# Weights of v and u of the first head pair loaded with q's and k's, and convolution parameters read as the twelfth step, in a hybrid decoder step

## The chip, the core and the metric

The kernel runs on one core of a Trainium2 chip. It is written in a tile framework whose scheduler decides, ahead of the run, in which order each engine's instructions stand; at run time every engine works through its own queue in that order. The engines are TensorE (PE, matrix products; its weight loads are shown as PEld), VectorE (DVE), ScalarE (ACT), GpSimd (POOL) and SyncE (SP), which issues nearly all DMAs. The metric is the device time of one execution in microseconds (us). Before the change the median of three runs is 2768.96 us (2768.74 to 2772.76).

## What is computed

One step of a decoder layer for a prompt of 2048 tokens (with 16 meta tokens ahead of it) and for 8 sampled tokens with paged caches. A normalised input h goes through one projection into q, k, v (8 heads of 64) and u (512 channels); q, k and v feed a stick-breaking attention, u a pooling mixer; their outputs go through one output projection, and a gated FFN with a causal convolution of width 3 follows.

```python
h = rmsnorm(xp, norm_mix_g)
q, k, v, u = project_mix(h, w_in)          # h @ w_in, cut into four
k_prompt, v_prompt = k, v                  # also outputs
...
o_attn = stick_breaking(q, k, v, ...)      # A = sigmoid(z) * prod(1 - sigmoid(z)), z = q k^T * scale + bias
o_pool = multiscale_pool(u, 0, T, pool_w, pool_scale)
xp = xp + concat([o_attn, o_pool]) @ w_out
h2 = rmsnorm(xp, norm_ffn_g)
f, conv_prompt = conv_ffn(h2, zero_prefix, w_up, conv_w, conv_b, w_down)
y_prompt = rmsnorm(xp + f, norm_final_g)
```

## The kernel before

All is float32. A product is done as three products of split values: `split` (L159) casts a tile to a high part on ScalarE (L160) and subtracts on VectorE for the low part (L161); `mm3` (L163) then runs high x high, high x low and low x high (L166 to L168).

**The input projection** is tiled by g, one of four head pairs (128 channels each of q, k, v and u), and by ch, one of four chunks of 512 tokens. `prep_first` loads the four x tiles of chunk 0 (`xt`), squares them (L209), works out 1/rms (`rstd_from`), scales them on VectorE (L232), and `turned` transposes them (`tpx`, L222) into eight tiles `hk` with high and low part (L225, L226), which are also written to DRAM (`hs_s`, L228). For chunks 1 to 3 the same is done in two parts while g is 0: `prep_squares` loads and squares four x tiles (`xt`, rooms shared with the attention's `om`), and `prep_piece` loads a quarter of the columns again as `xp` (L259), scales and turns it. `prep_small` does it for the 24 rows of sampled and meta tokens.

`step(g, ch, ki)` projects one of q, k, v, u (ki 0 to 3) for one g and ch. With ch 0 and ki 0 or 2 it first calls `load_w` for two kinds (the weights `wr`, two rooms, split into `wh` and `wl`), and `few_rows`, which multiplies the 24 small rows by the unsplit weights (L302), turns the result (`tq`, L307) and writes it out. `project` runs 24 products of 512 columns into one of two banks (`psm`), copies them out (`kf`, L384) and writes q and k to DRAM (`q_s`, `k_s`, L386); k and v are turned once more (`pk`, L353) and go to the outputs from `ko` (L357). For u the window sums become `dT`. At ch 1, ki 3, `fold_pool` multiplies the pooling's weights into part of w_out (`pkf`, `pkw`, L395 and L402, with a tile `wt` of w_out), and scales with one column group of `par`.

`room` (L195) gives one of four shared tiles (`kf`, `sm`, `qt`, `dT`, `wt` and others).

**The attention** runs in units of a block of 128 queries and up to 512 keys. `fetch` reads k and q back from DRAM (`raw` and `qr`, L469, L457, L458; `vtm` and `vt` for v, L481, L487; six `vt` rooms of 256 KB) and splits them; `chain` computes `z` (L518), two sigmoids (L519, L520) and a scan along the keys on VectorE (L527), `turn` transposes and `weigh` multiplies by v (`po`, L615).

**The order** is set in two ways. A list `fill` holds the steps of the input projection and, behind them, those of the output projection. Between attention units as many steps of `fill` are called as the next units need, and at least as many as spread the list's input part evenly over three quarters of the units. `with_params`, the second of `fill`, reads the convolution's parameters and the pooling's scale (`ra`, `rb`; turned as `pkp`, L636, L637, into `par`) and the state of the pooling (`sp`; turned as `pkg`, L642, and summed into `spool`). In that order of calls the framework's scheduler then places the instructions on the engines, by its own estimate of when each is ready.

The convolution's part of `par` is not read before the FFN; `fold_pool` reads the pooling's scale from it; `few_rows` for v and u reads `spool`.

Of the kernel before, what the change touches and what calls it, by code (L numbers as in the profile page):

```python
# [9 lines left out]
F32 = mybir.dt.float32  # L10
# [4 lines left out]
ALU = mybir.AluOpType  # L15
# [46 lines left out]
def hymba_kernel(  # L62
# [96 lines left out]
    def split(hi, lo, src):  # L159
        nc.scalar.copy(hi, src)  # L160
        nc.vector.tensor_tensor(out=lo, in0=src, in1=f32(hi), op=ALU.subtract)  # L161
# [122 lines left out]
        nc.vector.tensor_tensor(out=hsml[:, :, 0:n], in0=tp[:, :, 0:n], in1=gcol.unsqueeze(2).broadcast_to([P, NK, n]),  # L284
                                op=ALU.mult)

    def load_w(g, kind):
        ft = 4 * "qkvu".index(kind) + g
        wr = pa.tile([P, NK, P], F32, name="wr", bufs=2)
        nc.sync.dma_start(out=wr, in_=w_in[:, ft * P:(ft + 1) * P].rearrange("(c p) f -> p c f", p=P))  # L290
        wh = pa.tile([P, NK, P], F32R, name="wh", bufs=4)
        wl = pa.tile([P, NK, P], F32R, name="wl", bufs=4)
        split(wh, wl, wr)
        return wh, wl, wr

    def few_rows(g, pair, w):

        cs = slice(g * P, (g + 1) * P)
        ps = tt_tile("t24")[:, 0, :]
        for c in range(NK):  # L300
            for j in range(2):
                nc.tensor.matmul(ps[32 * j:32 * j + 32, :], hsml[:, c, :], w[pair[j]][2][:, c, :],  # L302
                                 start=c == 0, stop=c == NK - 1, skip_group_check=True)
        sm = room("sm")[:64, 0:P]
        nc.scalar.copy(sm, ps[:64, :])
        tq = tt_tile("tq")[:, 0, 0:64]
        nc.tensor.transpose(tq, sm, ident[:64, :64])  # L307
        mt = pb.tile([P, P], F32, name="mt", tag="ot")[:, 0:64]
        nc.vector.tensor_copy(mt, tq)
        if pair == "qk":  # L310
            qt = room("qt")[:NS, 0:P]
            nc.vector.tensor_scalar(out=qt, in0=sm[0:NS, :], scalar1=SCALE, scalar2=None, op0=ALU.mult)
            nc.sync.dma_start(out=qd_s[:, cs], in_=qt)
            nc.sync.dma_start(out=k_sample[:, cs], in_=sm[32:32 + NS, :])
            nc.sync.dma_start(out=k_prompt[0:META, cs], in_=sm[32 + NS:32 + NS + META, :])
            nc.sync.dma_start(out=q_s[g][:, 0:META], in_=mt[:, NS:NS + META])
            nc.sync.dma_start(out=k_s[g][:, 0:META], in_=mt[:, 32 + NS:32 + NS + META])
            return
        nc.sync.dma_start(out=v_sample[:, cs], in_=sm[0:NS, :])
        nc.sync.dma_start(out=v_prompt[0:META, cs], in_=sm[NS:NS + META, :])  # L320
        nc.sync.dma_start(out=pool_sample[:, 14, cs], in_=sm[32:32 + NS, :])
        us, um = mt[:, 32:32 + NS], mt[:, 32 + NS:32 + NS + META]
        ut = pa.tile([P, META], F32, name="utail", bufs=2)
        tails[g] = ut
        nc.vector.tensor_copy(ut, um)
        ub = room("ubm")
        nc.vector.memset(ub[:, 0:META], 0.0)
        nc.vector.tensor_copy(ub[:, META:2 * META], um)
        src = window_sums(ub, g, 2 * META)
        dT = room("dTm")  # L330
        nc.vector.tensor_tensor(out=src[:, META:2 * META], in0=src[:, META:2 * META], in1=invc[:, g, :], op=ALU.mult)
        nc.vector.tensor_tensor(out=dT[:, NS:NS + META], in0=src[:, META:2 * META], in1=um, op=ALU.subtract)
        nc.vector.tensor_tensor(out=dT[:, 0:NS], in0=spool[:, g, :], in1=us, op=ALU.add)
        nc.vector.scalar_tensor_tensor(out=dT[:, 0:NS], in0=dT[:, 0:NS], scalar=1.0 / WIN[g], in1=us,
                                       op0=ALU.mult, op1=ALU.subtract)
        nc.sync.dma_start(out=cat_s[4 + g, :, 0:NS + META], in_=dT[:, 0:NS + META])
# [67 lines left out]
            nc.scalar.copy(wf, pk)  # L404
            nc.sync.dma_start(out=wf_s[g * P:(g + 1) * P, q * CW:(q + 1) * CW], in_=wf)

    w = {}

    def step(g, ch, ki):

        pair = "qkvu"[ki // 2 * 2:ki // 2 * 2 + 2]
        if ch == 0 and ki % 2 == 0:
            for kind in pair:
                w[kind] = load_w(g, kind)
            few_rows(g, pair, w)
        nxt = (ch + 1) % NCH
        ahead = ki == 3 and (g < 3 if ch == NCH - 1 else g > 0)
# [207 lines left out]
            if end:  # L625
                end()

    def with_params():
        ra, rb, sp = room("ra")[:, 0:P], room("rb")[:NPR - P, 0:P], room("sp")[:15 * NS, 0:512]
        cw = conv_w.rearrange("i (f p) -> (i f) p", p=P)  # L630
        nc.sync.dma_start(out=ra, in_=cw[0:P, :])
        nc.sync.dma_start(out=rb[0:4, :], in_=cw[P:132, :])
# [3 lines left out]
        nc.tensor.transpose(tp[:, 0:P], ra, ident)  # L636
        nc.tensor.transpose(tp[:, P:NPR], rb, ident[:NPR - P, :NPR - P])  # L637
        nc.vector.tensor_copy(par, tp)
        nc.sync.dma_start(out=sp, in_=state_pool.rearrange("b j f -> (b j) f"))
        for g, w in enumerate(WIN):  # L640
            tg = tt_tile("pkg").rearrange("p a b -> p (a b)")[:, 0:15 * NS]
            nc.tensor.transpose(tg, sp[:, g * P:(g + 1) * P], ident[:15 * NS, :15 * NS])  # L642
            nc.vector.tensor_reduce(out=spool[:, g, :],
                                    in_=tg.rearrange("p (b j) -> p b j", j=15)[:, :, 16 - w:],
                                    axis=AX.X, op=ALU.add)


    wo, out_pool = [], {}
# [48 lines left out]
    for fn, key in in_steps():  # L697
        fill.append(fn)
        if key:
            ready[key] = len(fill)  # L700
        if len(fill) == 1:
            fill.append(with_params)
    n_in = len(fill)
    fill += [lambda c=c: load_out(c) for c in range(NK)]
    heads = [attention(hp) for hp in range(4)]
# [547 lines left out]
```

## Time and profile before

| | us |
|---|---|
| median of 3 runs | 2768.96 (2768.74 to 2772.76) |
| the profiled execution: whole time | 2771.54 |
| the profiled execution: span, first to last instruction | 2769.8 |
| TensorE busy | 2662.7 (96%) |
| VectorE / ScalarE / GpSimd busy | 1805.2 / 1031.4 / 721.7 |

The mean granted clock of TensorE is 0.988 of its full speed. By stretches the input projection and the attention take the first 890 us or so, and the output projection's last tiles, the FFN and the sampled rows the rest, in which TensorE is busy for 1859 of 1880 us.

A row of a timeline is: start, length, engine, line, operation, output<-input, partitions x elements, and in brackets how long the engine was idle before the row and what it waited for. SPq is the queue of DMA issues on SP: its start is the time of the issue, not of the landing.

### The profile page before, as it was taken

The numbers are of one execution on the slowest core, as the hardware profiler recorded it, in microseconds if no ns is written. First come the engines' busy times: TensorE is split into PE (matmuls) and PEld (weight loads), VectorE is DVE, ScalarE is ACT, GpSimd is POOL, SyncE is SP. The second block draws the span as 40 slices with busy tenths as digits, with TensorE's granted clock in tenths as the row PEclk, the third lists the DMA queues.
The fourth block names the chain that finished last, engine by engine and source line by source line (L and its number), as shares of the span: only waits on it lengthen the run. The fifth ranks groups of instructions, "written<-read, shape, count | busy, mean of one in ns | idle before, by whom it ended". The sixth has DMA issues, their size and how long they took to land.

```text
span 2769.8 us, 39760 instructions
## 1 busy us (share of the span) xinstructions
PE 2662.7 (96%) x14759; PEld 2089.6 (75%) x14759; DVE 1805.2 (65%) x3037; ACT 1031.4 (37%) x1833; POOL 721.7 (26%) x736
## 2 busy tenths in 40 slices
PE   5899999999998999999999999999999999999998
PEld 4677777787786888778877777777776777777776
DVE  4588768857669588669977777777774541114434
ACT  4466656655557256423322222222222320012111
POOL 0012212211122011145554554445554200000000
PEclk9899999999999999999999999999999999999999
DMA  7653552454425433455556555646656574666551
GB/s 252 218 178 118 167 179 97 130 203 136 165 87 171 159 117 101 147 193 193 184 208 242 207 201 213 227 165 237 215 206 237 173 258 165 200 205 212 179 194 64
DMA packets 326375, 498.79 MB, mean 180 GB/s; under 512 B 25367, under 2 KB 238631, under 8 KB 309781
## 3 DMA queue, kind: packets, MB, share of 16 engines
q1 hardware_dynamic: 307749, 362.03, 39.8%
q0 software_dynamic: 18432, 134.23, 12.7%
q8 instruction: 116, 1.90, 0.3%
q14 instruction: 78, 0.64, 0.1%
HBM read 395.99 MB, written 100.59 MB: 179 GB/s over the span
## 4 chain that ended last, share of the span: by engine, by line
PE 79%; DVE 3%; issue 2%; DMA 2%; ACT 1%; POOL 0%; SPq 0%; DVEq 0%; ACTq 0%; POOLq 0%
PE psu L166 12%; PE psu L167 12%; PE psu L168 12%; PE psd L166 6%; PE psd L168 6%; PE psd L167 6%; PE po L615 4%; PE z L518 3%; PE tt L572 3%; PE dav L950 2%; PE psm L166 2%; PE psm L168 2%; PE psm L167 2%; PE pso L167 2%; PE pso L166 2%; PE pso L168 2%
## 5 line engine op out<-in xcount | busy, mean ns | idle before, releaser
L166 PE MATMUL psu<-h2c,uwh 128*128 128x512 f32 x1408 | 555.0, 394 | 4.0 <-ACT uwh L160 2.2
L168 PE MATMUL psu<-h2c,uwl 128*128 128x512 f32 x1408 | 550.7, 391 | 1.3 <-DVE uwl L161 1.3
L167 PE MATMUL psu<-h2c,uwh 128*128 128x512 f32 x1408 | 551.6, 392 | 0.0
L534 POOL TENSOR_TENSOR be<-be,om 128x512 f32<-128x512 f32 (+3 forms) x176 | 182.6, 1037 | 844.2 <-DVE om L529 302.0
L1048 DVE SCALAR_TENSOR_TENSOR cv<-psu,par,cv 128x511 f32<-128x511 f32 x352 | 261.2, 742 | 146.5 <-ACT cv L1045 142.9
L166 PEld LDWEIGHTS psu<-h2c,uwh 128*128 128x128 f32 x1408 | 265.2, 188 | 81.1 <-issue 10.9
L1059 POOL TENSOR_TENSOR cv<-cv,cv 128x512 f32<-128x512 f32 x88 | 224.7, 2554 | 388.6 <-DVE cv L1053 290.7
L168 PEld LDWEIGHTS psu<-h2c,uwl 128*128 128x128 f32 x1408 | 265.3, 188 | 63.7 <-issue 7.3
L167 PEld LDWEIGHTS psu<-h2c,uwh 128*128 128x128 f32 x1408 | 265.3, 188 | 62.1 <-issue 8.5
L529 DVE TENSOR_TENSOR_SCAN om<-om,zero 128x513 f32<-128x513 f32 (+1 forms) x224 | 274.0, 1227 | 46.2 <-ACT om L519 41.2
L519 ACT ACTIVATE om<-z,nbias 128x512 f32<-128x512 f32 (+5 forms) x360 | 213.3, 593 | 138.3 <-PE z L518 83.4
L1045 ACT ACTIVATE cv<-psu,par 128x512 f32<-128x512 f32 x176 | 136.4, 776 | 289.1 <-PE psu L168 289.1
L1220 DVE TENSOR_TENSOR xt<-psd,xt 128x512 f32<-128x512 f32 x64 | 44.0, 691 | 281.8 <-PE psd L168 281.7
L520 ACT ACTIVATE be<-z,bias 128x512 f32<-128x512 f32 (+5 forms) x360 | 211.4, 589 | 0.6 <-PE tt L572 0.6
L167 PE MATMUL psm<-hk,wh 128*128 128x512 f32 x512 | 206.6, 404 | 2.9 <-DVE hk L226 2.9
L166 PE MATMUL psm<-hk,wh 128*128 128x512 f32 x512 | 205.0, 406 | 1.9 <-ACT hk L225 1.3
L168 PE MATMUL psm<-hk,wl 128*128 128x512 f32 x512 | 204.2, 399 | 1.0 <-DVE wl L161 1.0
L161 DVE TENSOR_TENSOR uwl<-uwr,uwh 128x1024 fp32r<-128x1024 f32 x94 | 121.1, 1290 | 127.8 <-ACT uwh L160 127.8
L166 PE MATMUL psd<-wd,ah 128*128 128x512 f32 x512 | 200.3, 395 | 0.0
L167 PE MATMUL psd<-wd,ah 128*128 128x512 f32 x512 | 200.0, 392 | 0.0
L168 PE MATMUL psd<-wd,al 128*128 128x512 f32 x512 | 199.4, 390 | 0.0
L160 ACT CAST uwh<-uwr 128x1024 fp32r<-128x1024 f32 x94 | 98.8, 1054 | 246.4 <-PE psu L167 230.4
(245 smaller groups left out, 4773.8 us busy)
## 6 DMA issues: line engine op xcount, KB each, us to landing
hk<-hs_s SPq DMA_DIRECT2D x96, 512.0 KB
uwr<-in_w_up_dram SPq DMA_DIRECT2D x88, 512.0 KB
act_s<-sg SPq DMA_DIRECT2D x88, 256.0 KB
ar<-act_s SPq DMA_DIRECT2D x32, 704.0 KB
raw<-in_w_up_dram SPq DMA_DIRECT2D x40, 512.0 KB
xt<-in_x_prompt_dram SPq DMA_DIRECT2D x32, 512.0 KB
hs_s<-hk SPq DMA_DIRECT2D x32, 512.0 KB
uwr<-in_w_down_dram SPq DMA_DIRECT2D x22, 512.0 KB
```

The costliest lines, as they stand in the source:

```text
L161: nc.vector.tensor_tensor(out=lo, in0=src, in1=f32(hi), op=ALU.subtract)
L166: nc.tensor.matmul(ps, ah, bh, start=i == 0, stop=False)
L167: nc.tensor.matmul(ps, ah, bl, start=False, stop=False)
L168: nc.tensor.matmul(ps, al, bh, start=False, stop=i == n - 1)
L519: nc.scalar.activation(out=om[:M, e, 0:n], in_=z[:M, :n], func=AF.Sigmoid, scale=-SCALE, bias=nbias[:M, h:h + 1])
L520: nc.scalar.activation(out=be[:M, e, 0:n], in_=z[:M, :n], func=AF.Sigmoid, scale=SCALE, bias=bias[:M, h:h + 1])
L529: nc.vector.tensor_tensor_scan(out=rv, data0=rv, data1=zero[:M, 0:1].broadcast_to([M, n + 1]), initial=st["prev"][:M, e, 0:1], op0=ALU.mul ...
L534: (nc.gpsimd if cnt["mul"] % 2 == 0 else nc.vector).tensor_tensor(out=be[:M, e, m0:n], in0=be[:M, e, m0:n], in1=om[:M, e, m0 + 1:n + 1], o ...
L615: mm = nc.tensor.matmul(o, v_, a_, start=start, stop=stop, skip_group_check=True).ins
L1045: nc.scalar.activation(out=t, in_=ps, func=AF.Identity, scale=cpar(2, fi), bias=cpar(3, fi))
L1048: nc.vector.scalar_tensor_tensor(out=t[:, o:], in0=ps[:, 0:CW - o], scalar=cpar(d, fi), in1=t[:, o:], op0=ALU.mult, op1=ALU.add)
L1059: nc.gpsimd.tensor_tensor(out=cv[1], in0=cv[0], in1=cv[1], op=ALU.mult)
```

## The change

The weights of v and u of the first head pair (g = 0) are no longer fetched when v's step begins, but right behind those of q and k, in the first step, and they don't use the two `wr` rooms: each is fetched in two halves of 256 KB into rooms of the attention's value tiles `vt`. `load_w` is cut into `load_raw_w` (the DMA) and `split_w` (cast and subtraction, by halves for these two). `with_params` is cut in two: `pool_sums` (the pooling's state) stays the second in the list, and `conv_params` (`ra`, `rb`, `par`) is put in as number thirteen, behind the second `prep_squares`, so that every later step stands one place further back than if it had been left whole.

```diff
-    def load_w(g, kind):
+    def load_raw_w(g, kind):
+
         ft = 4 * "qkvu".index(kind) + g
+        wi = w_in[:, ft * P:(ft + 1) * P].rearrange("(c p) f -> p c f", p=P)
+        if (g, kind) in ((0, "v"), (0, "u")):
+            wr = [pb.tile([P, 4, P], F32, name="vt", bufs=VTB) for _ in range(2)]
+            for i in range(2):
+                nc.sync.dma_start(out=wr[i], in_=wi[:, 4 * i:4 * i + 4, :])
+            return wr
         wr = pa.tile([P, NK, P], F32, name="wr", bufs=2)
-        nc.sync.dma_start(out=wr, in_=w_in[:, ft * P:(ft + 1) * P].rearrange("(c p) f -> p c f", p=P))
+        nc.sync.dma_start(out=wr, in_=wi)
+        return [wr]
+
+    def split_w(wr):
         wh = pa.tile([P, NK, P], F32R, name="wh", bufs=4)
         wl = pa.tile([P, NK, P], F32R, name="wl", bufs=4)
-        split(wh, wl, wr)
-        return wh, wl, wr
+        n = NK // len(wr)
+        for i, src in enumerate(wr):
+            split(wh[:, n * i:n * i + n, :], wl[:, n * i:n * i + n, :], src)
+        return wh, wl, lambda c: wr[c // n][:, c % n, :]
...
     def step(g, ch, ki):
 
         pair = "qkvu"[ki // 2 * 2:ki // 2 * 2 + 2]
         if ch == 0 and ki % 2 == 0:
             for kind in pair:
-                w[kind] = load_w(g, kind)
+                w[kind] = split_w(raw_w.pop(kind) if (g, kind) in ((0, "v"), (0, "u")) else load_raw_w(g, kind))
+            if (g, ki) == (0, 0):
+                raw_w.update({kind: load_raw_w(0, kind) for kind in "vu"})
             few_rows(g, pair, w)
...
-    def with_params():
-        ra, rb, sp = room("ra")[:, 0:P], room("rb")[:NPR - P, 0:P], room("sp")[:15 * NS, 0:512]
+    def pool_sums():
+        sp = room("sp")[:15 * NS, 0:512]
+        nc.sync.dma_start(out=sp, in_=state_pool.rearrange("b j f -> (b j) f"))
+        for g, w in enumerate(WIN):
...
+    def conv_params():
+        ra, rb = room("ra")[:, 0:P], room("rb")[:NPR - P, 0:P]
...
         if len(fill) == 1:
-            fill.append(with_params)
+            fill.append(pool_sums)
+        if len(fill) == 12:
+            fill.append(conv_params)
```

The names that carry the same tile have other numbers in the two kernels, and lines behind L287 are moved by up to 19.

**ScalarE at the start of the program**, behind the squares of chunk 0's x tiles (`sq` is a square, `ss_403` and `ss_405` the sums of chunk 1, `wh` a weight's high part, `hk` chunk 0's turned tiles). Before:

```order
L209 ACTIVATE sq,ss<-xt 24x1024
L160 CAST wh<-wr 128x1024 x2
L209 ACTIVATE sq,ss_405<-xt 128x1024 x3
L225 ACTIVATE hk<-tpx,gcol 128x512
L209 ACTIVATE sq,ss_405<-xt 128x1024
```

And now:

```order
L209 ACTIVATE sq,ss<-xt 24x1024
L160 CAST wh<-wr 128x1024 x2
L160 CAST wh<-vt 128x512 x4
L209 ACTIVATE sq,ss_403<-xt 128x1024 x3
L225 ACTIVATE hk<-tpx,gcol 128x512 x3
```

The four casts of v's and u's halves stand ahead of chunk 1's squares and of the first `hk`. On VectorE the four subtractions that belong to them stand inside the steps of `rstd_from` for chunk 0.

**TensorE behind the small rows of q and k** (`t` is their product, `tq` its transpose, `psm` the next projection, which is v's in both). Before:

```order
L302 MATMUL t_323<-wr,hsml 32x128 x16
L307 MATMUL tq<-ident,sm 128x64
L636 MATMUL pkp<-ident,ra 128x128
L166 MATMUL psm<-hk,wh 128x512
L167 MATMUL psm<-hk,wh 128x512
```

And now:

```order
L314 MATMUL t_331<-wr,hsml 32x128 x16
L319 MATMUL tq<-ident,sm 128x64
L166 MATMUL psm<-hk,wh 128x512
L167 MATMUL psm<-hk,wh 128x512
L168 MATMUL psm<-hk,wl 128x512
```

The transpose of the parameters is gone from here; it now stands behind 21 products of v's projection in chunk 1.

**SP's queue between the q tiles of the first attention units and chunk 1's `xp`** (`qr` q tiles, `ko` the rows of k or v on their way out, `out_2` and `out_3` the outputs of k and v, `wr` the weights of the next head pair). Before:

```order
L457 DMA qr_599<-q_s0_57 64x256
L458 DMA qr_599<-q_s0_57 64x256
L457 DMA qr_909<-q_s0_57 64x256
L458 DMA qr_909<-q_s0_57 64x256
L259 DMA xp_625<-in_x_prompt_dram 128x4x256
L259 DMA xp_684<-in_x_prompt_dram 128x4x256
L259 DMA xp_708<-in_x_prompt_dram 128x4x256
L259 DMA xp_732<-in_x_prompt_dram 128x4x256
L357 DMA out_2_dram<-ko_473 128x4x128
L457 DMA qr_916<-q_s0_57 64x256
L458 DMA qr_916<-q_s0_57 64x256
L290 DMA wr_2942<-in_w_in_dram 128x8x128
```

And now:

```order
L332 DMA out_3_dram<-sm_503 16x128
L333 DMA out_8_dram<-sm_503 8x128
L348 DMA cat_s_65<-dTm_519 128x24
L495 DMA vtm_571<-out_3_dram 16x64 x2
L471 DMA qr_597<-q_s0_57 64x256
L369 DMA out_3_dram<-ko_557 128x4x128
L472 DMA qr_597<-q_s0_57 64x256
L259 DMA xp_623<-in_x_prompt_dram 128x4x256
L393 DMA cat_s_65<-dT_679 128x512
L501 DMA vt_570<-out_3_dram 128x3x128
L259 DMA xp_682<-in_x_prompt_dram 128x4x256
L259 DMA xp_706<-in_x_prompt_dram 128x4x256
```

The small rows and the tiles of v, which stood behind the four `xp`, now stand ahead of them and between them; the two weights of the next head pair, which stood behind, are issued far earlier, the first ahead of q's and k's small rows, the second ahead of k's write to `k_s`.

Further on, at the first `fold_pool`, the second `wt` on SP stood behind two `xt` of `prep_squares` and now stands ahead of the second of them. From about 465 us on the steps stand at other places among the attention units, up to 890 us; the FFN's order is the same.

More of the change, by code (lines that the diff above doesn't have):

```diff
@@ L301, in few_rows @@
             for j in range(2):
-                nc.tensor.matmul(ps[32 * j:32 * j + 32, :], hsml[:, c, :], w[pair[j]][2][:, c, :],
+                nc.tensor.matmul(ps[32 * j:32 * j + 32, :], hsml[:, c, :], w[pair[j]][2](c),
                                  start=c == 0, stop=c == NK - 1, skip_group_check=True)
@@ L405, in fold_pool @@
             nc.sync.dma_start(out=wf_s[g * P:(g + 1) * P, q * CW:(q + 1) * CW], in_=wf)
-    w = {}
+    w, raw_w = {}, {}
     def step(g, ch, ki):
@@ L626, in weigh @@
                 end()
-    def with_params():
-        ra, rb, sp = room("ra")[:, 0:P], room("rb")[:NPR - P, 0:P], room("sp")[:15 * NS, 0:512]
+    def pool_sums():
+        sp = room("sp")[:15 * NS, 0:512]
+        nc.sync.dma_start(out=sp, in_=state_pool.rearrange("b j f -> (b j) f"))
+        for g, w in enumerate(WIN):
+            tg = tt_tile("pkg").rearrange("p a b -> p (a b)")[:, 0:15 * NS]
+            nc.tensor.transpose(tg, sp[:, g * P:(g + 1) * P], ident[:15 * NS, :15 * NS])
+            nc.vector.tensor_reduce(out=spool[:, g, :],
+                                    in_=tg.rearrange("p (b j) -> p b j", j=15)[:, :, 16 - w:],
+                                    axis=AX.X, op=ALU.add)
+    def conv_params():
+        ra, rb = room("ra")[:, 0:P], room("rb")[:NPR - P, 0:P]
         cw = conv_w.rearrange("i (f p) -> (i f) p", p=P)
@@ L638, in with_params @@
         nc.vector.tensor_copy(par, tp)
[L639 to L645, printed above, removed]
     wo, out_pool = [], {}
```

## The prediction

> **What bounds the kernel now.** I read the page first, then the busy time by stage, then TensorE's rows in order of time.
>
> ```profile
> span 2769.8 us, 39760 instructions
> PE 2662.7 (96%) x14759; PEld 2089.6 (75%) x14759; DVE 1805.2 (65%) x3037; ACT 1031.4 (37%) x1833; POOL 721.7 (26%) x736
> ```
>
> TensorE is busy for 96% of the span, so only time in which TensorE stands still can be won. The busy time of TensorE by stage (columns: the stretch, its length, PE busy and its instructions, granted clock, DMA share, GB/s):
>
> ```profile
> 0.00:39.00 39.00, 19.65 (x122) 1.00 0.85 295
> 39.00:78.00 39.00, 23.39 (x124) 0.75 0.59 177
> ...
> 92.00:135.00 43.00, 33.97 (x157) 0.88 0.60 197
> ...
> 465.00:890.00 425.00, 399.24 (x2788) 0.98 0.43 142
> ```
>
> Before 39 us TensorE waits for inputs; from 39 to 78 us it stands for 15.6 us, at a mean granted clock of 0.75; from 92 to 135 us for 9.0 us. The change works in these three stretches. TensorE's timeline, with the idle time before a row and its releaser in brackets:
>
> ```profile
> 22.05 0.73 PE L166 MATMUL psm<-hk,wh 128*128 128x512 f32 x2 [1.31 <-ACT hk L225]
> ...
> 38.91 0.27 PE L307 MATMUL tq<-ident,sm 64*128 64x64 f32 x1 [0.38 <-ACT sm L305]
> 45.30 0.45 PE L636 MATMUL pkp<-ident,ra 128*128 128x128 f32 x1 [6.12 <-DMA ra<-in_conv_w_dram]
> 45.40 0.77 PE L166 MATMUL psm<-hk,wh 128*128 128x512 f32 x1
> ...
> 48.53 0.43 PE L167 MATMUL psm<-hk,wh 128*128 128x512 f32 x1
> ...
> 59.34 0.39 PE L168 MATMUL psm<-hk,wl 128*128 128x512 f32 x1
> ...
> 60.68 1.94 PE L302 MATMUL t<-wr,hsml 128*32 128x128 f32 x32
> ...
> 71.15 0.70 PE L518 MATMUL z<-kst,qh 128*128 128x400 f32 x1 [6.02 <-ACT qh L160]
> 74.27 0.70 PE L518 MATMUL z<-kst,ql 128*128 128x400 f32 x1 [2.42 <-DVE ql L161]
> ...
> 78.03 1.20 PE L166 MATMUL psm<-hk,wh 128*128 128x512 f32 x2
> ```
>
> q and k of chunk 0 are projected from 22.05 us, v and u from 45.40 to 59.7 us; at 78.03 us chunk 1 begins, which is my marker. Two waits stand out: 6.12 us for the convolution parameters, and 6.02 + 2.42 us for a q tile. Seven products from 45.40 to 48.53 us are spaced at 0.45 us; 48 products in 14.2 us with transposes between them (22.05 to 36.3 us) are spaced at some 0.23 us, so the clock after the wait costs 7 x 0.22 = 1.5 us.
>
> **Term 1: the start, +3.8 us.** The v and u weights now stand ahead of chunk 1's x tiles on SP and their casts ahead of those tiles' squares on ScalarE. ScalarE before:
>
> ```profile
> 10.03 1.06 ACT L209 ACTIVATE sq<-xt 128x1024 bf16<-128x1024 f32 x1 [0.81 <-DMA xt<-in_x_prompt_dram]
> ...
> 13.83 1.04 ACT L160 CAST wh<-wr 128x1024 fp32r<-128x1024 f32 x1 [0.68 <-DMA wr<-in_w_in_dram]
> ...
> 15.12 1.06 ACT L209 ACTIVATE sq<-xt 128x1024 bf16<-128x1024 f32 x1 [0.24 <-DMA xt<-in_x_prompt_dram]
> ...
> 20.27 1.06 ACT L209 ACTIVATE sq<-xt 128x1024 bf16<-128x1024 f32 x1 [2.69 <-DMA xt<-in_x_prompt_dram]
> ...
> 21.32 0.67 ACT L225 ACTIVATE hk<-tpx,gcol 128x512 fp32r<-128x512 f32 x1
> ```
>
> The two weights of q and k, 1 MB, came 3.8 us behind the last tile of chunk 0 (13.83 - 10.03). Another 1 MB in the same pieces takes another 3.8 us, so the tile squared at 15.12 comes at 18.9 us. Its square frees the room of the third tile, which was squared 5.15 us behind (20.27 - 15.12); that becomes 24.1 us. The first hk stands behind this third square on ScalarE as it did before, so it starts at 25.1 instead of 21.32 us, and so does TensorE's first product, 25.8 for 22.05. VectorE's path is no later:
>
> ```profile
> 14.91 1.22 DVE L161 TENSOR_TENSOR wl<-wr,wh 128x1024 fp32r<-128x1024 f32 x1 [0.37 <-ACT wh L160]
> ...
> 17.03 2.74 DVE L232 TENSOR_SCALAR xt<-xt,rr 128x1024 f32<-128x1024 f32 x4
> ```
>
> Four half-size wl now stand inside the chain that makes r, with which the tiles were scaled from 17.03 us. The last quarter of the weights lands near 17.6, its cast and wl take half of 1.04 and of 1.22 us, the small steps left 1 us: 19.8 us, +2.8. This also is all that the split into eight half-size casts and subtractions costs. Bounds of the term: 0, if the weights ride in idle DMA time, and 4.5 us.
>
> ```profile
> 14.00:16.00 2.00, 0.00 (x0) 0.00 (x0) 1.63 (x4) 1.75 (x2) 0.00 (x0) 1.00 1.02 410
> 16.00:18.00 2.00, 0.16 (x1) 0.16 (x2) 2.00 (x13) 1.42 (x4) 0.00 (x0) 1.00 0.55 176
> ...
> 20.00:22.00 2.00, 0.73 (x4) 0.33 (x3) 0.60 (x1) 1.73 (x4) 0.09 (x1) 1.00 0.39 154
> ```
>
> The last two columns (DMA share, GB/s) say why I take 3.8: where the weights now stand the engines are full (1.02); the slack (0.55, 0.39) comes behind it, while the third tile is issued late. The Trainium skill (DMA: Bandwidth & Descriptors, Rules for kernel authors) says to issue a DMA early and to wait for it late; by it the start would cost nothing and the sum below be -9.1 us, which is rival B. Here the wait isn't late: the casts stand in front.
>
> **Term 2: the parameters' wait, -6.1 - 1.5 us, and +0.8 given back.** Behind tq the next row on TensorE is now v's first product, whose weights have been split long since. Both parts are needed for this: before, v's weights would not have let it start before 44.9 us either.
>
> ```profile
> 42.30 1.06 ACT L209 ACTIVATE sq<-xt 128x1024 bf16<-128x1024 f32 x1 [0.22 <-DMA xt<-in_x_prompt_dram]
> 43.85 1.04 ACT L160 CAST wh<-wr 128x1024 fp32r<-128x1024 f32 x1 [0.40 <-DMA wr<-in_w_in_dram]
> 45.05 0.58 ACT L384 COPY kf<-psm 128x512 f32<-128x512 f32 x1 [0.15 <-DMA q_s<-kf]
> ```
>
> So tq ends at 43.0 (39.2 + 3.8), and 48 products of 0.23 us follow without the slow clock. u needs k's bank, whose copy kf (45.05) stands behind two squares (the later at 42.30) whose tiles come some 5 us later (3.8, and one more hs_s write ahead of them): kf ends near 49.1, 0.5 us after v does. With 0.3 us for q's bank, u ends near 54.7; the sums' transposes, k's and the small product (1.94 us) end at 57.6 us.
>
> **Term 3: what is late next, 12.3 us of idle for 9.5.** From here the attention's first units wait for q and k to go out and come back, and chunk 1 for its xp tiles, all on SP's queue.
>
> ```profile
> 46.02 0.35 SPq L386 DMA_DIRECT2D k_s<-kf  x1
> 50.08 1.18 SPq L469 DMA_DIRECT2D raw<-k_s  x2
> ...
> 59.18 2.17 SPq L259 DMA_DIRECT2D xp<-in_x_prompt_dram  x4
> ```
>
> k_s goes out at 49.2 for 46.02 (+3.2), so the casts of the q tiles move alike:
>
> ```profile
> 56.27 0.20 ACT L160 CAST qh<-qr 128x16 fp32r<-128x16 f32 x1 [2.05 <-DMA qr<-q_s]
> 57.93 0.41 ACT L160 CAST qh<-qr 128x256 fp32r<-128x256 f32 x1 [1.45 <-DMA qr<-q_s]
> ```
>
> The second 16-wide z waits to 59.7 us (idle some 2 us), the first 144-wide z to 62.4 (another 2; its DMA stands behind ko). The second half of the next q tile (qr_597) stands behind vtm, which reads back what the small rows wrote, and behind v's ko:
>
> ```profile
> SPq L487 <- DMA out_dram<-ko: 6.0, 4, 3.4
> ...
> SPq L481 <- DMA out_dram<-sm: 2.7, 1, 2.7
> ```
>
> A read-back held SP for 2.7 us at vtm and up to 3.4 us at vt. With that qr_597 is complete at 65.6 us and its z starts near 68.3, an idle of about 5 us. xp_623 is issued at 66.2 for 59.18, and needs 3.5 us until VectorE scales it:
>
> ```profile
> 62.71 1.14 DVE L232 TENSOR_SCALAR xp<-xp,rr 128x256 f32<-128x256 f32 x4 [0.46 <-DMA xp<-in_x_prompt_dram]
> ```
>
> xp_682 waits behind dT and vt (which waits for ko to land, 2.3 us), so it is scaled near 73 us, and chunk 1's first product runs at 74.2 us. Four z of 400 (0.70 us at half clock; 1.2 us in all at full clock, an estimate) and the parameters' transposes (0.5 us) now lie behind the marker: 74.2 + 1.7 = 75.9 against 78.03, **-2.1 us** for terms 1 to 3. Split up: start +3.8, idle 12.3 for 15.6, -3.3, and 1 us of slow clock for 3.6, -2.6. The Trainium skill (TensorE: Matmul & The Clock Gate, What's actually happening) states that the clock halves after an idle window of about 3.4 us and comes back after as long a busy one; the row behind the 6.12 us wait agrees (seven slow products in 3.1 us). By it the 5 us wait alone would cost half of such a window, 1.7 us for my 1, and the sum below would be -4.6 us, an estimate.
>
> **Term 4: the fold, -3.2 us.** The second pkw of the first fold waits for its wt tile:
>
> ```profile
> 116.45 3.88 SPq L87 DMA_DIRECT2D xt<-in_x_prompt_dram  x2
> 120.39 0.42 SPq L400 DMA_DIRECT2D wt<-in_w_out_dram  x1
> ```
>
> ```profile
> 124.54 2.04 PE L402 MATMUL pkw<-wt,pT 128*128 128x512 f32 x2 [3.97 <-DMA wt<-in_w_out_dram]
> ```
>
> wt stood behind two x tiles, the second held for a room until 120.3. Now it stands ahead of that second one: issued about 3 us earlier, and four products stand between the two pkw. 3.97 shrinks by 3.2; bounds 0 and 4.5 (with the slow clock behind it).
>
> **Term 5: other orders, 0 (-4 to +4).** One more step in the list shifts the steps between attention units by a place from 465 to 890 us. The idle there is 25.8 us (425 - 399.24), none of it in work that the change touches; a new order wins some of it and loses some, and I take a sixth of it for both ends.
>
> Sum: -2.1 - 3.2 = **-5.3 us**. The profiled execution took 2771.54 us (span 2769.8), 2.6 above the median of 2768.96; its span becomes 2764.5, and the median **2763.7 us**.
>
> **The rivals.**
> (A) No new waits: SP gets through the read-backs as fast as products end, 3 us of idle where I have 12.3. Gain 5.3 + 9.3 = 14.6, 2754.4 us. For it: the two weights of the next head pair, which stood behind the xp tiles, now go out long before. Against it: the order of SP.
> (B) The start costs nothing, because the weights ride in the slack at 16 to 24 us: 5.3 + 3.8 = 9.1, 2759.9 us. Against it: the share of 1.02.
> (C) All given back: xp_682 is 3.5 us later than I think, or the parameters' wait returns at step twelve (ra behind eight hs_s writes; up to 6.1 us, if it lands after TensorE has done 21 products of v): -5.3 + 3.5 to + 6.1, within 0.2%, 2767.2 to 2769.8 us. For it: every read-back in term 3 is a guess of a queue. Against the second: those 21 products are 4.8 us of cover.
> (D) Slower: SP's queue as the bound. Three read-backs (raw, vtm, vt) now stand ahead of xp, and a q tile that stood behind transfers of 2 MB made TensorE wait 6.02 us. Two such waits come to +12, in all +6.7 us, 2775.7 us. For it: term 3 is the sum of such waits already. Against it: between 39 and 78 us the engines moved data for 0.59 of the time. It decides where chunk 1 starts after 85 us (74.2 + 5.3 + 5.5).
>
> **How the numbers follow.** About 0.2%, 5.5 us, is what a measurement of this kernel can tell from no change; the line lies at 2763.4, just under my forecast. Forecast 0.48 (own range 2759 to 2768, with term 5: faster 0.22, same 0.26); A 0.12 and B 0.12, faster; C 0.20, same; D 0.08, slower. Faster 0.46, same 0.46, slower 0.08. The range reaches to A and C's ends: 2755 to 2771; it leaves out D and half of A, with a little of the rest.
>
> **What would show it.** Right: first product of chunk 0 near 25.8 us; no wait between tq and v; waits of 2 to 5 us at the 144-wide z and at tpx<-xp; chunk 1 at 74 us; pkw's wait under 1 us; pkp without a wait. Wrong: the first product still at 22 us (B); chunk 1 before 68 (A) or after 85 us (D); or a difference that arises only between 465 and 890 us.

## The result, and the profile after

| | median us | ratio to before, 95% interval |
|---|---|---|
| before (13 executions) | 2769.36 (2765.82 to 2772.76) | |
| after (13 executions) | 2775.24 (2769.87 to 2778.28) | 1.0017 (1.0010 to 1.0024) |

The change makes the kernel slower, by 0.08 to 0.17% in three comparisons: two later ones gave 1.0008 and 1.0012 (e10 and e16 below; e10's interval still holds 1). Forecast were 2763.7 us, and at most 2771. The profiled execution took 2777.46 us (span 2775.8), 2.2 above the median.

The first lines of the page after:

```profile
span 2775.8 us, 39754 instructions
...
PE 2667.2 (96%) x14759; PEld 2092.8 (75%) x14759; DVE 1807.1 (65%) x3039; ACT 1033.0 (37%) x1835; POOL 719.1 (26%) x736
```

TensorE is busy 4.5 us longer for the same 14759 instructions; where, is said below. Its busy time by stage (columns as before, with PEld, DVE, ACT and POOL behind PE):

```profile
0.00:39.00 39.00, 16.47 (x78) 12.70 (x79) 20.37 (x66) 21.96 (x36) 4.43 (x47) 0.96 0.85 286
39.00:78.00 39.00, 28.50 (x171) 22.29 (x170) 16.35 (x66) 14.71 (x35) 1.90 (x8) 0.83 0.67 207
...
92.00:135.00 43.00, 36.55 (x197) 27.09 (x195) 24.34 (x57) 21.35 (x46) 3.87 (x6) 0.92 0.68 219
...
465.00:890.00 425.00, 396.41 (x2760) 314.30 (x2758) 310.54 (x483) 253.69 (x530) 84.95 (x155) 0.98 0.43 142
```

Up to 39 us TensorE does 3.2 us less than before, in the next 39 us 5.1 more, in the fold's stretch 2.6 more: the start is paid for and won back with a gain. From 465 to 890 us it does 2.8 us less (396.41 for 399.24), far from any transfer that the change touches. TensorE's timeline after, at the places that the prediction named:

```profile
25.60 0.73 PE L166 MATMUL psm<-hk,wh 128*128 128x512 f32 x2 [1.93 <-ACT hk L225]
...
44.11 0.27 PE L319 MATMUL tq<-ident,sm 64*128 64x64 f32 x1 [0.39 <-ACT sm L317]
44.59 0.50 PE L166 MATMUL psm<-hk,wh 128*128 128x512 f32 x1 [0.21 <-ACT kf L396]
...
58.06 1.94 PE L314 MATMUL t<-vt,hsml 128*32 128x128 f32 x32 [1.38 <-DVE spool L648]
...
63.05 0.33 PE L532 MATMUL z<-kst,qh 128*128 128x144 f32 x1 [1.80 <-ACT qh L160]
...
68.30 0.49 PE L532 MATMUL z<-kst,qh 128*128 128x144 f32 x1 [4.00 <-ACT qh L160]
...
70.79 0.66 PE L222 MATMUL tpx<-ident,xp 128*128 128x128 f32 x2 [1.54 <-DVE xp L232]
...
74.83 1.20 PE L166 MATMUL psm<-hk,wh 128*128 128x512 f32 x2
...
96.16 0.27 PE L660 MATMUL pkp<-ident,ra 128*128 128x128 f32 x1
...
122.01 1.25 PE L414 MATMUL pkw<-wt,pT 128*128 128x512 f32 x2 [2.23 <-DMA wt<-in_w_out_dram]
```

The first product is at 25.6 us, the wait between `tq` and v's first product is gone, chunk 1 begins at 74.83 (before 78.03), `pkp` waits for nothing, and `pkw`'s wait has shrunk from 3.97 to 2.23 us. So far it went as forecast. A marker further on is `pku`, which turns the last columns of u once for each head pair; the rows of the tile's view (length in ns: least, median, most; first and last start in us), before and after:

```profile
L373 PE MATMUL pku<-ident,kf x4: 272/278/283, 277.0 to 840.3; 128*15 128x128 f32 x4
```

```profile
L385 PE MATMUL pku<-ident,kf x4: 272/273/283, 273.0 to 839.2; 128*15 128x128 f32 x4
```

At the end of the first pair's projection the changed kernel is 4.0 us ahead, at the end of the last pair's 1.1. The first product of the output projection (`pso`) starts at 859.3 us before and 861.6 after: 2.3 us behind. **Between the first `pku` and the first `pso`, 6.3 us were lost** (588.6 for 582.3). Most of that is waiting: in this stretch TensorE is idle for 28.8 us instead of 23.4, and busy for 1.0 us more. The experiments are read by this stretch. The other 3.7 us of the two spans' distance lie behind the first `pso` (1914.2 us to the end for 1910.5), with 3.4 of the 4.5 us of longer busy time, and are this execution's own: in two further profiles, e9 of before and e10 of after, that part took 1910.0 and 1910.4 us, and over all profiles here it lies between 1907.2 and 1914.2.

### The profile page after: what moved, and what is told of

Same layout as the page of the kernel before. It is cut to its first block, busy times and chain, and to the rows that moved or that the text cites. A ratio compares the mean times of both kernels' runs of the same rounds, so it can differ in the third digit from the quotient of the medians.

```text
span 2775.8 us, 39754 instructions
## 1 busy us (share of the span) xinstructions
PE 2667.2 (96%) x14759; PEld 2092.8 (75%) x14759; DVE 1807.1 (65%) x3039; ACT 1033.0 (37%) x1835; POOL 719.1 (26%) x736
## 4 chain that ended last, share of the span: by engine, by line
PE 78%; DVE 4%; DMA 2%; issue 2%; ACT 1%; POOL 0%; SPq 0%; DVEq 0%; ACTq 0%; POOLq 0%
PE psu L166 12%; PE psu L167 12%; PE psu L168 12%; PE psd L166 6%; PE psd L168 6%; PE psd L167 6%; PE po L629 4%; PE z L532 3%; PE tt L586 3%; PE psm L166 2%; PE psm L168 2%; PE psm L167 2%; PE dav L969 2%; PE pso L166 2%; PE pso L167 2%; PE pso L168 2%
## 5 line engine op out<-in xcount | busy, mean ns | idle before, releaser
L1067 DVE SCALAR_TENSOR_TENSOR cv<-psu,par,cv 128x511 f32<-128x511 f32 (+1 forms) x352 | 261.3, 743 | 148.1 <-ACT cv L1064 146.6
```

Source lines behind the costliest of these rows:

```text
L1067: nc.vector.scalar_tensor_tensor(out=t[:, o:], in0=ps[:, 0:CW - o], scalar=cpar(d, fi), in1=t[:, o:], op0=ALU.mult, op1=ALU.add)
```

## The experiments

Three theories stood at first. T: the added place in the list `fill` costs the time, whatever stands in it, since it moves later steps to other attention units. W: the weights in the `vt` rooms cost it. N: the gain of the start is given back anyway. By the list's arithmetic (one entry more in `n_in` and in all later `needs`) 17 of the projection's steps are called one attention unit later, none earlier: u of chunk 2 of the first pair, and 16 steps between the units 78 and 127 of 180.

**e1, the place alone.** The kernel before, with an entry that does nothing:

```diff
+        if len(fill) == 12:
+            fill.append(lambda: None)
```

> The kernel before with one entry that does nothing as number thirteen of the list; weights and parameters as before, so that only the places of later steps among the attention units move. Theory T (the added place in the list costs what the changed kernel lost behind 465 us): 2779 us, 2775 to 2783, level with the kernel before until 465 us, then +8 to +10. Theory W (weights in the vt rooms, or their transfers, cost it): 2769 us. Theory N (whatever is won at the start is given back by the attention's own pace): 2769 us.

Measured: 2777.12 us, ratio 1.0032 (1.0020 to 1.0044), first `pku` to first `pso` 587.1 us. An entry that does nothing costs more than the whole change does. T holds.

**e2, the change without the place.** The parameters are read inside the twelfth entry:

```diff
         if len(fill) == 12:
-            fill.append(conv_params)
+            twelfth = fill[-1]
+            fill[-1] = lambda: (twelfth(), conv_params())
```

> The changed kernel, but the parameters are read inside the twelfth entry, behind its prep_squares, and not as an entry of their own: the list is as long as before. T: 2765 us, 2762 to 2768, the 4 us won by 273 us kept to the end. W: 2775 us as the changed kernel. N: 2769 us.

Measured: 2765.05 us, ratio 0.9983 (0.9974 to 0.9992), stretch 581.7 us. The rest of the change is worth 4.7 us (0.0017 x 2770). For the two halves together N falls, and with it the prediction's rival C; W falls too.

**e3 and e4, its halves**, both without the place. e3 keeps `with_params` whole as the second entry and fetches the weights early; e4 leaves the weights as before and reads the parameters inside the twelfth entry.

```diff
 (e3)
-            fill.append(with_params)
+            fill.append(lambda: (conv_params(), pool_sums()))
```

> Only the weights' half of the change: v's and u's weights early in vt rooms, parameters and pooling sums together as the second entry, the list as long as before. T: first product near 25.6 us, pkp behind v's products without a wait, the fold's wait for wt (4 us) stays: 2767 us, 2763 to 2771. W: 2775 us. N: 2769 us.

> Only the parameters' half, inside the twelfth entry, the list as long as before; v's and u's weights late as before. T: first product at 22 us, v's first product still near 45 us because its weights come late (wait 5 to 6 us), the fold's wait shortened: 2765 us, 2761 to 2769. W: below 2769 us as well, since no weights stand in vt. N: 2769 us.

Measured: e3 2771.79 us, 1.0006 (0.9997 to 1.0015); e4 2764.08 us, 0.9980 (0.9971 to 0.9989). The parameters' half brings the whole gain; the weights alone bring none that can be told. e3 lies just above what T said of it (2763 to 2771), so for the weights alone N isn't excluded, though in e3's profile, one of its two quickest executions, the first `pku` is at 270.2 us, 6.8 ahead of before. e4's TensorE shows what wasn't foreseen:

```profile
22.49 1.22 PE L166 MATMUL psm<-hk,wh 128*128 128x512 f32 x2 [1.82 <-ACT hk L225]
...
45.54 0.80 PE L166 MATMUL psm<-hk,wh 128*128 128x512 f32 x1 [4.72 <-ACT wh L160]
```

Without the early weights v waits 4.72 us for its cast, but the first product is 3.1 us earlier, and chunk 1 begins no later than with them (69.05 us). Behind v, TensorE waits for other things: 1.32 us for a q tile, 1.58 for an `xp` tile, 3.38 for a `hk`.

**e5 and e6, is it lateness?** e5: two empty entries (26 steps later). e6: e4 with ten steps called one unit earlier. Here and below the list stays as it is and only the units of the calls differ:

```diff
+    def target(ui, k):
+        ns = [n + k if n > 12 else n for n in needs]
+        want = max(first + (n - first) * (ui + 1) // max(u - PF, 1) if u - PF > ui else n
+                   for u, n in enumerate(ns[:ui + 24]))
+        return max(want if ui else first, min(n_in + k, first + (n_in + k - first) * ui // END)) - k
...
+        fill_to(target(ui, -1 if ui >= per else 0))
```

> Before, with two entries that do nothing behind the twelfth: 26 projection steps are called one attention unit later than before (one of them two), where one entry moved 17. Lateness (L: every step that comes later shortens the lead of q, k and v over the units that need them, so the price grows with the number of places): about twice the price of one place, +10 to +13 us, 2780 to 2784 us. Chance meeting (A: the price depends on which steps meet which units, without a trend): anywhere from -4 to +10 us, and less than that of one place as likely as not.

> The parameters' half inside the twelfth entry (2764.1 us with the list as it was), and ten steps between the units 77 and 116 called one unit earlier than before; nothing else. L: 3 to 6 us better than 2764, 2758 to 2761. A: between 2760 and 2770. If the order as it was is already the best one by its tuning to these units, and any move loses: 2766 to 2770.

Here theory L (every later step costs) stands against A (it matters which steps meet which units). Measured: e5 2772.06 us, 1.0010 (1.0001 to 1.0020), stretch 581.7; e6 2764.37 us, 0.9982 (0.9971 to 0.9993), stretch 579.3 (e4 579.4). Two places cost less than one, and ten steps earlier win nothing. L falls, A stands.

**e7 and e8, the 16 steps in two groups**, in the kernel before: `target(ui, 1 if per <= ui < 2 * per else 0)` and `target(ui, 1 if 2 * per <= ui else 0)`.

> Before, with only those five steps one unit later that the added place delays during the second head pair's attention (units 78 to 88: one of the second pair and four of the third). L: 5 of 16 delayed steps, +1.5 to +2.5 us. A: the whole price, +5 to +6.5 us, sits either here or in the other eleven, and the other run has none: a guess from the profile of the empty entry, whose lag against before is the same at 461 and at 677 us and grows behind it, is that it isn't here: 0 (-1 to +1).

> Before, with only those eleven steps one unit later that the added place delays during the third head pair's attention (units 90 to 127: seven of the third pair, four... of the last). L: 11 of 16, +3.5 to +4.5 us. A: the whole price, +5 to +6.5 us, as the lag of the empty entry grows behind 677 us, or none.

Measured: e7 2775.40 us, 1.0017 (1.0007 to 1.0027), stretch 583.8; e8 2771.98 us, 1.0009 (0.9999 to 1.0018), stretch 582.3. The guess that the first group is free misses: by the ratios it has about half of the price of e1 (1.0032), and the second about a quarter, with no change still inside its interval. L misses too, as the five steps cost more than the eleven.

**e9, e10, e11: the same programs again**, before, after and e1, to see whether the stretch is a matter of the program or of the execution.

> The kernel before once more, against itself: the ratio is 1.000, and its distance from 1 is what such a comparison can be wrong by. Its profile shows how much the stretch from the first pku (277 us) to the first pso (859.3 us), 582.3 us in the first profile, differs from one execution to the next of the same program. If the added place costs 5 us or more there by itself (T), this stays between 581 and 584 us; if such differences are the luck of an execution (R), it may come anywhere from 579 to 589.

> The changed kernel once more. T: ratio 1.0010 to 1.0025 again, and 587 to 590 us from the first pku to the first pso (588.6 in the first profile). R: the ratio stays, as it comes from many executions, but this stretch falls to 582 to 585 us and something else is long.

> Before with one entry that does nothing, once more. T: ratio 1.002 to 1.004, and 586 to 589 us from the first pku to the first pso (587.1 in its first profile). R: ratio between 1.000 and 1.003, the stretch 581 to 585 us.

Measured: e9 2770.03 us, 1.0000 (0.9991 to 1.0010), stretch 579.4 us; e10 2772.48 us, 1.0008 (0.9998 to 1.0017), 589.4 us; e11 2779.28 us, 1.0038 (1.0024 to 1.0053), 587.9 us. The stretch is the program's: 587.1 to 589.4 with the place in four profiles, 579.3 to 582.3 in the seven of the old order (before, e2, e3, e4, e6, e9 and e12 below; e6 differs by its ten steps). The idle time of TensorE in it goes along: 27.7 to 28.9 us with the place, 21.9 to 24.0 in the old order. e9 was a little under its expected 581 to 584, and e10's ratio a little under its 1.0010.

**e12, the weights behind the x tiles**, without the place: e2 with `raw_w.update` not in the first step but at the start of the k step, which puts v's and u's weights behind two x tiles of chunk 1 on SP's queue.

```diff
-            if (g, ki) == (0, 0):
-                raw_w.update({kind: load_raw_w(0, kind) for kind in "vu"})
             few_rows(g, pair, w)
+        if (g, ch, ki) == (0, 0, 1):
+            raw_w.update({kind: load_raw_w(0, kind) for kind in "vu"})
```

> The changed kernel without the added place (the parameters inside the twelfth entry), and with v's and u's weights asked for at the start of the k step, so that they stand behind the first two x tiles on SP's queue instead of ahead of them. If the later start of chunk 0 is a cost by itself (the prediction's +3.8 us): first product at 22 us again, no wait between tq and v, and 2 to 4 us better than 2765 us, so 2761 to 2763. If what the start wins is given back in the first chunk, as its idle time is set by SP's read-backs: 2764 to 2766.

Measured: 2770.29 us, 1.0001 (0.9991 to 1.0011): neither expectation. The profiled execution (2764.32 us, one of its two quickest) shows what was meant:

```profile
21.18 0.73 PE L166 MATMUL psm<-hk,wh 128*128 128x512 f32 x2 [0.35 <-ACT hk L225]
...
41.84 0.50 PE L166 MATMUL psm<-hk,wh 128*128 128x512 f32 x1 [0.21 <-ACT kf L396]
...
68.90 1.20 PE L166 MATMUL psm<-hk,wh 128*128 128x512 f32 x2
```

The start's cost is gone, the wait stays away, chunk 1 begins 9 us earlier than before; yet the median isn't better than before. Its ten executions reach from 2763.99 to 2775.66 us, and those of e3, whose profile is quick too, from 2767.15 to 2774.07. The record has the granted clock of each execution, and in e12 it goes with the time: 0.990 in the mean of the four quickest (up to 2766.24 us), 0.987 in that of the six longer ones, a difference that comes to some 7 us of 2770, an estimate from these figures. Why the clock was lower in those isn't in these profiles and stays open.

**The place near 600 us.** In all four profiles with the place, and in e5 and e8, TensorE stands at one row that has no such wait in the seven of the old order and in e7. TensorE after, at the start of the third pair's attention:

```profile
596.81 0.19 PE L596 MATMUL ttm<-ident,bm 16*32 16x16 f32 x1
596.93 0.44 PE L586 MATMUL tt<-ident,be 128*128 128x128 f32 x2
600.03 0.28 PE L596 MATMUL ttm<-ident,bm 128*32 128x128 f32 x1 [2.66 <-DVE atm L579]
600.07 0.47 PE L166 MATMUL psm<-hk,wh 128*128 128x512 f32 x1
...
601.35 0.63 PE L167 MATMUL psm<-hk,wh 128*128 128x512 f32 x1
601.77 0.63 PE L168 MATMUL psm<-hk,wl 128*128 128x512 f32 x1
...
606.10 0.49 PE L365 MATMUL pk<-ident,kf 128*128 128x128 f32 x3
```

The `ttm` at 600.03 needs a bank that still holds the small `ttm` of 596.81, until that is copied to `atm`. VectorE after:

```profile
595.20 1.36 DVE L541 TENSOR_TENSOR_SCAN om<-om,unseen 128x257 f32<-128x257 f32 x1
596.66 0.43 DVE L548 TENSOR_TENSOR be<-be,om 128x256 f32<-128x256 f32 x1
597.00 0.69 DVE L541 TENSOR_TENSOR_SCAN om<-om,unseen 128x257 f32<-128x257 f32 x1
597.61 2.31 DVE L543 TENSOR_TENSOR_SCAN om<-om,zero 128x401 f32<-128x401 f32 x2
599.84 0.14 DVE L579 COPY atm<-ttm 32x16 f32<-32x16 f32 x1
```

A copy of 0.14 us stands behind 2.8 us of the mask's scans (597.00 to 599.84), and behind the waiting `ttm` on TensorE stand 19 projection products, which then run without a wait of their own. In e2, with the old order, seven of these products stand between the small `ttm` and the next transposes, and cover it:

```profile
598.59 0.18 PE L596 MATMUL ttm<-ident,bm 16*32 16x16 f32 x1
598.70 0.50 PE L166 MATMUL psm<-hk,wh 128*128 128x512 f32 x1
...
600.19 0.40 PE L166 MATMUL psm<-hk,wh 128*128 128x512 f32 x1
600.43 0.27 PE L586 MATMUL tt<-ident,be 128*128 128x128 f32 x1
```

Behind the wait eight products (600.92 to 603.91) run at a spacing of 0.43 instead of 0.23 us. The granted clock (last but two columns) is halved from 600.74 to 604.15 us; this window, and the one of the same length ahead of it, after:

```profile
597.33:600.74 3.41, 0.75 (x5) 0.63 (x5) 2.98 (x5) 1.77 (x5) 1.33 (x2) 1.00 0.44 163
600.74:604.15 3.41, 3.41 (x10) 2.63 (x9) 0.68 (x2) 0.57 (x2) 0.98 (x2) 0.50 0.34 113
```

Half a clock over 3.4 us costs 1.7 us, so the place would cost 2.66 + 1.7 = 4.4 us at most. From this came theory M: this wait with its slow clock is the price, or most of it; and its rival S: what is won here is lost again behind it.

**e13, e14, e15: M against S.** The only delayed step ahead of this place that carries the third pair's fold is u of its chunk 1 (unit 93 for 92). e13 is the changed kernel with that one step back, e14 the kernel before with that step alone late, e15 the changed kernel in its own order, with the one 32x16 copy on ScalarE:

```diff
 (e13, on after)
+        fill_to(target(ui, -1 if ui == 92 else 0))
 (e14, on before)
+        fill_to(target(ui, 1 if ui == 92 else 0))
 (e15, on after)
-                on_act = cnt["at"] % 4
+                on_act = cnt["at"] % 4 or (hp == 2 and bi < 0)
```

> The changed kernel with one of its 17 delayed steps, u of the third head pair's second chunk with the fold behind it (unit 93), called at unit 92 again. If the wait of 2.66 us at ttm near 600 us and the slow clock behind it are what the place costs (M): both gone, 3 to 4.5 us off 2774, so 2769 to 2771. If the price is spread over the delayed steps (S): at most 1 us off.

> The kernel before with this one step called at unit 93 instead of 92, and nothing else. M: the wait of 2.66 us (1.9 to 2.7) at ttm near 600 us is there, with half a clock behind it, and the time is 3 to 4.5 us above 2770. S: no such wait or no such price, within 1 us of before.

> The changed kernel in its own order, with one instruction on another engine: the copy of the third head pair's first ttm (32x16) on ScalarE instead of VectorE, where it stands behind scans. M: no wait at ttm near 600 us, the clock stays at full speed there, 2.5 to 4.4 us off 2774, so 2769.5 to 2771.5, and 4 us off the lag at the following units. S: the wait goes, but comes back as another within 10 us; the time stays within 1 us of 2774.

Measured: e13 2768.13 us, 0.9991 (0.9981 to 1.0000), stretch 582.3, no wait; e15 2771.00 us, 1.0010 (1.0000 to 1.0020), stretch 586.1, no wait; e14 2770.74 us, 1.0001 (0.9991 to 1.0011), stretch 584.8. e14 has the wait, shorter, and its clock stays at 1.00:

```profile
601.78 0.28 PE L582 MATMUL ttm<-ident,bm 128*32 128x128 f32 x1 [1.75 <-DVE atm L565]
```

So the step makes the wait, but the price that M gives it isn't there without the others. e15's 2771.00 us lies in M's range, but its ratio lay between the two of the changed kernel, and was measured apart from them, so it decided nothing.

**e16, e17, e18: side by side**, the changed kernel, e15 and e13 again, with more executions.

> The changed kernel a third time, as the measure of the next two: ratio 1.0008 to 1.0017 as in its first two comparisons, and the wait of 2.66 us at ttm near 600 us with half a clock behind it.

> The changed kernel with the one 32x16 copy on ScalarE, beside e16. M (the wait and its slow clock are worth what they take on TensorE): 2.5 to 4.4 us under e16. S (what is won there is lost again behind it, and the first profile of this kernel was one of its quick executions): within 1 us of e16.

> The changed kernel with u of the third head pair's second chunk called one unit earlier, beside e16. M: 3 to 4.5 us under e16, as the same wait goes; S: within 1 us of it. If it is again 5 to 6 us under it, this step's place costs by more than that one wait.

| | median us | ratio to before | first `pku` to first `pso` |
|---|---|---|---|
| e16, after | 2773.69 (2772.36 to 2776.35) | 1.0012 (1.0003 to 1.0020) | 588.1 |
| e17, copy on ScalarE | 2769.95 (2767.25 to 2774.90) | 1.0001 (0.9992 to 1.0010) | 586.5 |
| e18, one step back | 2769.24 (2765.40 to 2772.94) | 0.9996 (0.9988 to 1.0005) | 583.9 |

e17 is 3.7 us under e16, e18 4.5: M's numbers, though the executions of e16 and e17 overlap. e16 has the wait again (2.67 us). TensorE in e17 at the same rows:

```profile
596.47 0.19 PE L596 MATMUL ttm<-ident,bm 16*32 16x16 f32 x1
596.59 0.44 PE L586 MATMUL tt<-ident,be 128*128 128x128 f32 x2
597.22 0.29 PE L596 MATMUL ttm<-ident,bm 128*32 128x128 f32 x1 [0.19 <-ACT atm L579]
597.75 0.50 PE L166 MATMUL psm<-hk,wh 128*128 128x512 f32 x1 [0.25 <-ACT kf L396]
...
602.21 0.49 PE L365 MATMUL pk<-ident,kf 128*128 128x128 f32 x3
```

From the small `ttm` to `pk` it takes 5.74 us (602.21 - 596.47) for 9.29 (606.10 - 596.81) in the changed kernel: 3.55 us by one copy of 0.14 us. The medians say 3.7, but the stretch is only 1.6 us shorter than e16's. The two traces settle it: e17 is 0.8 us behind e16 at the small `ttm` (596.47 for 595.70), 2.8 ahead at `pk` (602.21 for 604.98) and still 2.9 ahead at the last `pku` (835.1 for 838.0). What is won stays won there, against S; the rest of the stretch's difference was lost ahead of the wait and behind the last `pku`.

## Why the prediction was wrong

**Terms 1 to 4 were right in their sum.** Without the place the change measures -4.7 us (-2.2 to -7.2) for -5.3. The first `pku` is at 277.0 us in the mean of the eight profiles with the old start (before, e1, e5, e7, e8, e9, e11, e14) and at 271.9 in the eight with the whole change's start (after, e2, e10, e13, e15 to e18): -5.1 us. By the same means the lead is 1.4 us at the start of u in chunk 1 (97.3 for 98.6 us; terms 1 to 3 were to give 2.1), and 4.4 behind the first fold, at the start of k in chunk 2 (133.8 for 138.2).

- *Term 1, the start:* +3.8 forecast, +3.55 measured (25.60 for 22.05; 2.9 in the means of the eight and eight profiles). Rival B (no cost) is refuted for this order of the queues; e12 shows that the cost is the order, not the fetch: behind the first two x tiles of chunk 1, and with their casts behind these tiles' squares, the same weights cost the start nothing. The Trainium skill (DMA: Bandwidth & Descriptors, Rules for kernel authors) says to issue a DMA early and to wait for it late, which the prediction weighed as a start without cost; after's trace says 3.55 us, as x tiles that were needed sooner stood behind it.
- *Term 2, the parameters:* both waits went as said. But "both parts are needed" holds for the wait alone, not for the time: e4, with the parameters' half, gains as much.
- *Term 3, what is late next:* the 144-wide z waits were 1.80 and 4.00 us for about 2 and 5, the latter row at 68.30 us for 68.3, the 16-wide one 0.39 for about 2, `tpx` 1.54; chunk 1's first product at 74.83 for 74.2. Not foreseen were 1.38 us of `t` behind the sums. A (no new waits) and D (chunk 1 behind 85 us) didn't happen, though D's time, 2775.7, came out by another way.
- *Term 4, the fold:* -3.2 forecast; the wait itself shrank by 1.7 (2.23 for 3.97), but from the start of chunk 2 to its second projection, which spans the fold, the mean lead grew from 1.6 to 4.4 us, by 2.8.

**Term 5 failed: "other orders, 0 (-4 to +4)".** The place costs 0.0025 to 0.0034 of 2770 us in the changed kernel (after's three ratios against e2's), 7 to 9 us, and 9 to 11 us in the kernel before (e1 and e11). The term took idle time as what a new order shifts about, and a sixth of it as the end of the range. Two things were left out. An engine works off its rows in order, so that moving a step by one unit doesn't only move its work but uncovers rows that it had covered; here a 0.14 us copy behind scans came to stand between TensorE and 19 products. And a wait of 2.7 us cost up to another 1.7 by the clock, in the five profiles of the place though not in e5. The prediction had named the sign by which this would show, a difference that arises only between 465 and 890 us, but gave it a range instead of a rival of its own.

**What stays open.** Of the 7 to 9 us, one wait accounts for some 3.5: e17's trace shows it, and the medians beside e16 agree, though e15, measured apart, says less. All five profiles with the place (e1, e11, and after's three) have three more waits; TensorE after:

```profile
532.89 1.12 PE L365 MATMUL pk<-ident,kf 128*128 128x128 f32 x4 [1.90 <-ACT kf L396]
...
687.78 0.50 PE L168 MATMUL psm<-hk,wl 128*128 128x512 f32 x1 [1.41 <-DVE wl L161]
...
708.32 0.66 PE L365 MATMUL pk<-ident,kf 128*128 128x128 f32 x4 [2.80 <-ACT kf L396]
```

The first is 1.4 to 1.9 us in these five, the second 1.4, and neither is there in the old order; the third is 2.1 to 2.9 us for 1.1 to 1.4. With 2.7 us at `ttm` that is some 7 us of waiting more than in the old order, against 5 to 6 us of idle time that the place adds in all. In e17 all three remain; in e13 and e18 the second and the third are gone too, which fits that e18 wins the more. But no run moved one of these three alone, so that they make up the rest of the price is argued, not shown, and a wait needn't cost what it lasts: in e14 the third is 4.38 us, and e14 is no slower than before.

The five steps delayed during the second pair's attention cost some 5 us by themselves (e7, ratio 1.0017); of these waits e7's profile has the first alone, 1.38 us. Its ten executions also ran at a lower granted clock, 0.9871 in the mean for 0.9880 of the kernel before beside it, and why stays open. The parts don't add up either: e14's step alone costs nothing that can be measured, while taking it back wins 4.5 us (e18).

**The fastest version** is e4, 2764.08 us, 0.9980 (0.9971 to 0.9989): the parameters' half alone, read inside the twelfth entry. It beats both kernels. e2 and e6 can't be told from it.

## What to carry to other kernels

An entry in a list from which work is spread by counting is not free, even when it is empty: put new work inside a neighbouring entry first, and time the empty entry by itself (here +0.3%, more than the change could win, while two empty entries cost 0.1%). When work that covers others is moved, look at what it had covered: for each row that must wait, ask which engine releases it and what stands ahead of the release in that engine's queue. A short copy that frees a bank belongs on the engine that is free at that moment, and a profile of one execution proves a mechanism, not a gain of 0.1%; that takes medians side by side.

## What was not expected of the hardware

- The clock was halved though TensorE wasn't idle for a whole window: in the 3.41 us ahead of the slow stretch (597.33 to 600.74) it was busy for 0.75 us, 22%. The same wait of 2.66 us in e5 cost no clock. TensorE's row in e5:

```profile
602.69 0.28 PE L582 MATMUL ttm<-ident,bm 128*32 128x128 f32 x1 [2.66 <-DVE atm L565]
```

  The clock of e5 last changed at 372.06 us, and if windows run on from there, 67 of 3.413 us lead to about 600.75, into the midst of the wait (600.03 to 602.69). The length is after's: the slow stretch took 3.41 us, and the 68.27 us between its changes at 535.88 and 604.15 are twenty such lengths. The two windows that share it in e5, with a granted clock of 1.00:

```profile
597.34:600.75 3.41, 2.69 (x10) 1.31 (x9) 3.20 (x6) 3.19 (x7) 1.28 (x4) 1.00 0.24 80
600.75:604.16 3.41, 1.47 (x10) 1.33 (x11) 2.93 (x6) 1.84 (x5) 1.39 (x3) 1.00 0.58 217
```

  The Trainium skill (TensorE: Matmul & The Clock Gate, What's actually happening) says that the window runs freely, some 3.4 us long, and that an idle one halves the clock. The traces agree with the length, and e5 fits the free running; but a window that was 22% busy was enough. How busy a window must be isn't settled: the one ahead of e8's slow stretch was busy for 1.50 us, and e5's second, which kept the clock, for 1.47.
- The order of TensorE's rows decides to within 3 us: the stretch from the first `pku` to the first `pso` took 588.6, 589.4 and 588.1 us in three profiles of the changed kernel, and 582.3 and 579.4 in two of the kernel before, while whole executions of one program differ by 7 us (before) to 12 us (e12).
